# Down projection by Strassen's steps, in two phases of the feed-forward

## The chip, the cores and the metric

One core of a Trainium2 chip. The time is the device time of one execution in microseconds (us), as a median of several runs; the profile is of one execution. TensorE (PE) multiplies matrices, VectorE (DVE), ScalarE (ACT) and GpSimd (POOL) work elementwise, SyncE (SP) issues transfers; GpSimd and ScalarE can issue transfers too.

## The reference

One layer of a streaming encoder on x (512 positions, 1024 features, float32). What the change touches is the channel mixer at its end; everything is float32.

```
x = x + W_o (sigmoid(g_A) * y_A + sigmoid(g_B) * y_B)      # mixer before it
h = rms_norm(x, norm_ffn_g)
up = causal_dwconv(h @ w_up, conv_ffn_w)                   # 1024 -> 2 x 2816, 3 taps
a, b = split(up)
x = x + (silu(a) * b) @ w_down                             # 2816 -> 1024
return rms_norm(x, norm_f_g)
```

## The kernel before

Everything lies transposed: features on the 128 partitions, the 512 positions along the free axis. A matrix is a grid of 128 x 128 blocks; `w_down` has 22 blocks along its 2816 inputs (`k`) and 8 along its 1024 outputs (`j`).

To be exact enough, each float32 operand is split into a high half (rounded to the type that TensorE takes at speed) and a low half, the remainder. `mm3` (lines 175 to 187) forms a product from three matmuls, high by high, low weight by high, high by low, each cut to 256 columns; so a block of 512 positions takes 6 matmuls and one of 256 takes 3. All sums are in PSUM, in eight banks of 512 columns.

Weights come as one stream of chunks, `stream`, each 128 x 1024 at most (8 blocks). `load` issues a chunk's transfer on SP's queue, `AHEAD` chunks ahead of use, into a ring of `AHEAD` + 1 raw buffers. `split` makes the halves: ScalarE copies the raw chunk into the high half (line 154), VectorE subtracts that from the raw chunk (line 158), which is the remainder. There are two buffers for each half, so the split of a chunk waits until TensorE has done with the chunk two before it. `chunk` hands the halves out in order.

A planner (the language's scheduler) sets the order of the instructions on each engine: among those that it expects to be ready, the one that the program has first. It is held by `keep`, which keeps program order for all matmuls and SP's loads, and by `after_split`, which puts a block's instructions behind the last split on their engine.

The feed-forward: the loop over `j` in 0..21 takes two up blocks each (`a` and `b`), multiplies each by the norm's factor (line 724), convolves (`taps`: one scaled copy on ScalarE, two multiply-adds on VectorE), applies silu (line 729), multiplies on GpSimd (line 730), and splits the product into `gh` and `gl` (lines 731 and 732). Then, for each of the 8 output blocks, `down` accumulates 22 blocks from three chunks into one PSUM bank; VectorE adds the bank to `x1` (line 761), ScalarE squares and scales it, GpSimd sums the squares (line 653). The last output block is done in two halves of the positions, so that the first half's norm and output run beside the second half's matmuls (`fin_sum`, `fin_col`, `fin_out`); `warm_on` gives TensorE matmuls without a use while the last norm is worked out.

Of the kernel before, what the change touches and what calls it, by code (L numbers as in the profile page):

```python
# [24 lines left out]
AHEAD = 3  # L25
# [4 lines left out]
PADL, PADR = 48, 120  # L30
# [6 lines left out]
RC = 2 * (S + H)  # L37
WC = D + P
WOFF = {"h": 0, "l": 32}
# [3 lines left out]
def block_kernel(ctx, tc, xT, vecs, wv, win, wmix, wo, wup, wdn, outT):  # L43
# [28 lines left out]
    def col(i):  # L72
        return vec[:, i : i + 1]
# [42 lines left out]
    stream += [(f"up{j}", wup[j], D) for j in range(2 * NP)]  # L116
    for j in range(KB):
        for c in range(3):
            a, b = 8 * c * P, min(8 * c + 8, NP) * P
            stream.append((f"dn{j}{c}", wdn[j, :, a:b], b - a))  # L120
    raws, parts, order = [], [], {}

# [7 lines left out]
    def load(upto):  # L130
        for k in range(len(raws), min(upto, len(stream) - 1) + 1):
            nm, src, ncol = stream[k]
            raw = wp.tile([P, RC], F32, tag="raw", name=f"raw_{nm}", bufs=AHEAD + 1)[:, :ncol]

            keep((nc.scalar if k == 0 else nc.sync).dma_start(raw[:, : VW if k == 0 else ncol], src[:, : VW if k == 0 else ncol]))
            if k == 0:
                keep(nc.sync.dma_start(raw[:, VW:], src[:, VW:]))
            raws.append(raw)

    def split(hl=None):  # L140

        k = len(parts)
        if k == len(stream):
# [3 lines left out]
        hi, lo = hl or [  # L147
            wp.tile([P, WC], F32R, tag=f"w{x}", name=f"w{x}_{nm}", bufs=2)[:, WOFF[x] : WOFF[x] + ncol] for x in "hl"
        ]
        if k == 0:  # L150
            for cs in (slice(0, VW), slice(VW, S + H)):
                keep(nc.vector.tensor_copy(hi[:, cs], raws[k][:, cs]))
        else:
            ins = nc.scalar.activation(hi, raws[k], AF.Copy)  # L154
# [3 lines left out]
        ins = nc.vector.tensor_sub(lo, raws[k], hi.bitcast(F32))  # L158
# [87 lines left out]
    ssq = cp.tile([P, S], F32, tag="ssq", name="ssq1")  # L246
# [398 lines left out]
    ssq2 = cp.tile([P, S], F32, tag="ssq", name="ssq2")  # L645
# [57 lines left out]
    gh = fp.tile([P, NP, S], F32R, tag="gh", name="gh")  # L703
    gl = fp.tile([P, NP, S], F32R, tag="gl", name="gl")

    acc = ring(*range(6))
    rb2 = None
    for j in range(NP):
        uu = []
        if j == 0:  # L710
            nrm = {}

            def mid():
                nrm["c"] = rstd_col([ssq2], NT, 6, "n2")

            def late():
# [179 lines left out]
```

## Time and profile before

| | |
|---|---|
| median of 3 runs | 726.09 us (725.95 to 726.13) |
| the profiled execution | 725.93 us, span 724.1 us |
| mean granted TensorE clock | 0.996 |
| TensorE busy | 715.0 us (99%), 6231 matmuls |
| VectorE, ScalarE, GpSimd busy | 398.6, 293.6, 129.6 us |
| read from HBM, written | 68.29 MB, 2.10 MB |

A row of a group of instructions has the line, the engine, the operation, what is written and read, shapes and count; then the busy time, the mean of one in ns, and the engine's idle time before them with what ended it. A row of the timeline has start and duration in us, then the same, with the idle time before it in brackets. A row of stages has the length, the busy time and count of PE, weight loads (PEld), DVE, ACT and POOL, the granted clock, the busy share of the DMA engines, and GB/s. A row of the chain has start, duration and what ran.

### The profile page before, as it was taken

Reading aid. Unit: us, or ns where it says so; the run is one execution under the profiler, and the core shown is the slowest. Engines: PE = TensorE matmul, PEld = TensorE weight load, DVE = VectorE, ACT = ScalarE, POOL = GpSimd, SP = SyncE. Lnnn points to the kernel's source line nnn. Section 1 sums busy time; section 2 is a strip of 40 time slices with the busy share of each in tenths; the row PEclk is TensorE's granted clock in tenths of the full one; section 3 lists DMA queues with packets and bytes.
Section 4 is the critical chain, followed back from the end, with each engine's and each line's share of the span. In section 5 each row is a group of like instructions: output and inputs, shape, how many; then the busy total and the mean of one; then the engine's idle time right before and its main releaser. Section 6 shows DMA issues by size and latency. Waiting matters only on the chain.

```text
span 724.1 us, 14479 instructions
## 1 busy us (share of the span) xinstructions
PE 715.0 (99%) x6231; PEld 713.5 (99%) x6231; DVE 398.6 (55%) x588; ACT 293.6 (41%) x449; POOL 129.6 (18%) x145
## 2 busy tenths in 40 slices
PE   9999999999999999999999999999999999999996
PEld 9999999999999999999999999999999999999995
DVE  6677767655545445455376666666666663222322
ACT  6564545444332332334254434434434433223321
POOL 5124433222000000123311101101101100000102
PEclk9999999999999999999999999999999999999998
DMA  8523122221232332542233233333333333323303
GB/s 259 156 62 116 61 83 65 61 87 59 65 111 89 106 99 88 162 159 88 88 101 105 88 100 105 90 95 109 89 99 105 89 88 97 110 81 110 103 1 117
DMA packets 23360, 71.39 MB, mean 99 GB/s; under 512 B 2912, under 2 KB 5600, under 8 KB 23296
## 3 DMA queue, kind: packets, MB, share of 16 engines
q1 hardware_dynamic: 20992, 67.09, 30.3%
q0 software_dynamic: 896, 2.13, 0.9%
q10 hardware_dynamic: 1408, 1.24, 0.5%
q8 instruction: 49, 0.80, 0.5%
q14 instruction: 15, 0.12, 0.1%
HBM read 68.29 MB, written 2.10 MB: 97 GB/s over the span
## 4 chain that ended last, share of the span: by engine, by line
PE 95%; DVE 2%; ACT 1%; issue 1%; ACTq 0%; POOL 0%; DVEq 0%
PE p_up L183 33%; PE pd L183 14%; PE p_in L183 14%; PE p_wo L183 6%; PE p_gb L183 5%; PE p_ga L183 5%; PE yc L183 3%; PE ya L183 3%; PE o L183 2%; PE pa L307 2%; PE pb L309 2%; PE tp L473 1%; PE pdB L183 1%; PE pdA L183 1%; PE s L444 1%; PE s L445 1%
## 5 line engine op out<-in xcount | busy, mean ns | idle before, releaser
L183 PE MATMUL p_up<-x1h,wh_up 128*128 128x256 f32 x704 | 137.4, 276 | 0.0
L183 PE MATMUL p_up<-x1h,wl_up 128*128 128x256 f32 x704 | 137.0, 276 | 0.0
L183 PE MATMUL p_up<-x1l,wh_up 128*128 128x256 f32 x704 | 136.9, 276 | 0.0
L183 PEld LDWEIGHTS p_up<-x1h,wh_up 128*128 128x128 f32 x704 | 106.1, 188 | 0.0
L183 PEld LDWEIGHTS p_up<-x1h,wl_up 128*128 128x128 f32 x704 | 105.9, 188 | 0.0
L183 PEld LDWEIGHTS p_up<-x1l,wh_up 128*128 128x128 f32 x704 | 105.9, 188 | 0.0
L158 DVE TENSOR_TENSOR wl_in<-raw_in,wh_in 128x1024 fp32r<-128x1024 f32 x36 | 50.7, 1409 | 30.1 <-ACT wh_in L154 29.6
L730 POOL TENSOR_TENSOR fu<-fu,fu 128x512 f32<-128x512 f32 x22 | 28.4, 1291 | 211.2 <-DVE fu L402 198.3
L158 DVE TENSOR_TENSOR wl_up<-raw_up,wh_up 128x1024 fp32r<-128x1024 f32 x44 | 53.7, 1221 | 14.5 <-ACT wh_up L154 14.5
L183 PE MATMUL pd<-gl,wh_dn 128*128 128x256 f32 x308 | 60.0, 276 | 0.0
L183 PE MATMUL pd<-gh,wh_dn 128*128 128x256 f32 x308 | 60.0, 276 | 0.0
L183 PE MATMUL pd<-gh,wl_dn 128*128 128x256 f32 x308 | 59.9, 276 | 0.0
L183 PE MATMUL p_in<-xgh,wh_in 128*128 128x256 f32 x288 | 56.9, 279 | 1.1 <-DVE t_q L375 1.1
L183 PE MATMUL p_in<-xgl,wh_in 128*128 128x256 f32 x288 | 56.5, 277 | 0.0
L183 PE MATMUL p_in<-xgh,wl_in 128*128 128x256 f32 x288 | 56.4, 277 | 0.0
L158 DVE TENSOR_TENSOR wl_dn<-raw_dn,wh_dn 128x1024 fp32r<-128x1024 f32 (+1 forms) x23 | 26.0, 1132 | 54.9 <-ACT wh_dn L154 54.8
L154 ACT ACTIVATE wh_up<-raw_up 128x1024 fp32r<-128x1024 f32 x44 | 46.4, 1055 | 22.3 <-issue 13.4
L154 ACT ACTIVATE wh_in<-raw_in 128x1024 fp32r<-128x1024 f32 x36 | 38.2, 1060 | 42.5 <-PE ya L183 12.7
L154 ACT ACTIVATE wh_dn<-raw_dn 128x1024 fp32r<-128x1024 f32 (+1 forms) x23 | 22.7, 985 | 66.5 <-PE pd L183 66.1
L183 PEld LDWEIGHTS p_in<-xgh,wh_in 128*128 128x128 f32 x288 | 44.7, 188 | 1.9 <-ACT wh_in L154 1.3
L183 PEld LDWEIGHTS pd<-gl,wh_dn 128*128 128x128 f32 x308 | 46.4, 188 | 0.0
L183 PEld LDWEIGHTS pd<-gh,wh_dn 128*128 128x128 f32 x308 | 46.4, 188 | 0.0
(227 smaller groups left out, 1590.9 us busy)
## 6 DMA issues: line engine op xcount, KB each, us to landing
raw_up<-in_wup_dram SPq DMA_DIRECT2D x44, 512.0 KB, 3.6
raw_in<-in_win_dram SPq DMA_DIRECT2D x36, 512.0 KB, 3.5
raw_dn<-in_wdn_dram SPq DMA_DIRECT2D x16, 512.0 KB, 3.5
raw_mix<-in_wmix_dram SPq DMA_DIRECT2D x8, 512.0 KB, 3.6
raw_wo<-in_wo_dram SPq DMA_DIRECT2D x8, 512.0 KB, 5.6
raw_dn<-in_wdn_dram SPq DMA_DIRECT2D x8, 384.0 KB, 3.2
xr<-in_xT_dram POOLq DMA_DIRECT2D x8, 256.0 KB, 3.8
raw_v<-in_wv_dram SPq DMA_DIRECT2D x7, 260.0 KB, 5.4
```

The source lines that it names most:

```text
L154: ins = nc.scalar.activation(hi, raws[k], AF.Copy)
L158: ins = nc.vector.tensor_sub(lo, raws[k], hi.bitcast(F32))
L183: keep(nc.tensor.matmul(out[:, cs], w, x[:, cs], start=start and i == 0 and c == 0, stop=stop and i == 2 and c == len(cut) - 1,))
L307: keep(nc.tensor.matmul(pa[t][:, :VW], xt, w[:, :VW], start=start, stop=stop))
L309: keep(nc.tensor.matmul(pb[t], xt, w[:, VW:], start=start and t % 2 == 0, stop=stop and t % 2 == 1))
L444: keep(nc.tensor.matmul(s[:, :nn], QT[pr][:, e, qs], KA[pr][:, e, :nn], start=True, stop=False))
L445: keep(nc.tensor.matmul(s[:, :nn], QB[pr % 2][: KR[e], e, qs], KBt[pr % 2][: KR[e], e, :nn], start=False, stop=True))
L473: keep(nc.tensor.transpose(tp[:, ks], pt[:, ks], ident))
L730: nc.gpsimd.tensor_mul(a, a, b)
```

## The change

The feed-forward is done in two phases: hidden blocks 0 to 11, then 12 to 21. In each, the up projection is followed by that part of the down projection, added into `x1` in SBUF.

The down projection takes two output blocks (a pair `i` of rows), two hidden blocks (a pair `q`) and the two halves of the 512 positions as a 2 x 2 matrix product and forms it by seven products of 128 x 128 by 128 x 256 in place of eight, in Winograd's form of Strassen's method. That needs sums on both sides and a recombination:

- Hidden side, `glu`, once per pair `q`: four sums on VectorE (t1 to t4), then one copy and one remainder over all seven operands of 256 columns (eight in phase 1, which also keeps the plain ones).
- Weight side, once per step: five blocks are loaded (320 KB); a DMA issued from GpSimd adds two blocks of 128 KB from HBM onto the fourth and fifth (`add_in`); two GpSimd additions of 128 columns make the sixth and seventh (`sum_up`). `split` calls these one and two chunks ahead.
- Output side, `combine`, once per pair of rows and phase: seven VectorE operations and one ScalarE copy bring four banks' worth of products into two blocks of `x1`. In phase 1 the squares and the scaling follow, the sum of squares now on VectorE.

Phase 0 has 4 x 6 = 24 steps; phase 1 has 3 x 5 = 15, and output blocks 6 and 7 go there without Strassen's method, in three chunks (`dp0` to `dp2`), half by half for the end of the kernel. In each phase the steps of the first two pairs of rows are ordered so that the last two pairs `q` come late. The ring of raw buffers goes from 4 to 5, buffers `fz` from 3 to 2 and `fu` from 4 to 3. The transfer of weights is laid out for this on the host, by copying only.

```diff
-AHEAD = 3
+AHEAD = 4
+PHASES = ((0, 12), (12, NP))
...
+    for ph, (j0, j1) in enumerate(PHASES):
+        qs = list(range(j0 // 2, j1 // 2))
+        head, rest = qs[:-2], qs[-2:]
+        st = [(i, q) for part in (head, rest) for i in (0, 1) for q in part]
+        st += [(i, q) for i in ((2, 3), (2,))[ph] for q in qs]
...
+    def add_in(upto):
...
+                nc.gpsimd.dma_start(form(k, 3, 2), stream[k][1][:, : 2 * P], accum_op=ALU.add)
+    def sum_up(upto):
...
+                add_in(k)
+                nc.gpsimd.tensor_add(form(k, 5), form(k, 3), form(k, 1))
+                nc.gpsimd.tensor_add(form(k, 6), form(k, 5), form(k, 2))
...
     def split(hl=None):
...
         load(k + AHEAD)
+        sum_up(k + 1)
+        add_in(k + 2)
...
+    def glu(ph, j, uu):
...
+        nc.vector.tensor_sub(t1, b11, b12)
+        nc.vector.tensor_sub(t3, b22, b12)
+        nc.vector.scalar_tensor_tensor(t2, t1, -1.0, b22, op0=ALU.mult, op1=ALU.subtract)
+        nc.vector.scalar_tensor_tensor(t4, t2, -1.0, b21, op0=ALU.mult, op1=ALU.subtract)
+        gs, rs = slice(g0, g0 + NF + ph), slice(0, NF + ph)
+        nc.scalar.activation(gh[:, gs, :], graw[:, rs, :], AF.Copy)
+        nc.vector.tensor_sub(gl[:, gs, :], graw[:, rs, :], gh.bitcast(F32)[:, gs, :])
+    PROD = (
+        (1, 0, 2, 0), (2, 1, 0, 0), (6, 2, 0, 1), (0, 6, 1, 0), (3, 3, 1, 1), (5, 4, 2, 1), (4, 5, 3, 0),
+    )
+    def step(ph, i, q, banks, first, last):
+        wh, wl = chunk(f"st{i}_{q}")
...
+        for f, g, b, h in PROD:
...
+            mm3(banks[b][:, th[h]], wh[:, fs], wl[:, fs], gh[:, g0 + g, :], gl[:, g0 + g, :], ...)
...
+        split_next()
+    def split_next():
+        while len(parts) < chunk.n + 1 and len(parts) < len(stream):
+            if stream[len(parts)][0].startswith("dp"):
+                break
+            split()
+    def combine(ph, i, banks):
...
+        nc.scalar.activation(z[:, th[0]], p16[:, th[0]], AF.Copy)
+        nc.vector.tensor_add(m1, p23, m1)
+        nc.vector.tensor_sub(m2, m2, p45)
+        nc.vector.tensor_add(z[:, th[1]], p16[:, th[1]], z[:, th[0]])
+        nc.vector.tensor_add(u3, p7, z[:, th[1]])
+        nc.vector.tensor_add(m1[:, th[1]], p45[:, th[1]], m1[:, th[1]])
+        nc.vector.tensor_add(m1, m1, z)
+        nc.vector.tensor_sub(m2h, m2h, u3.unsqueeze(1).to_broadcast([P, 2, 2 * P]))
...
+    def down(ph, banksets):
...
+            step(ph, i, q, open_[i], first, last)
+            if last:
+                with after_split():
+                    combine(ph, i, open_[i])
...
+    for m in range(2):
+        plain(m, 0, kall)
+    sqA = [fin_sum(0, 0), fin_sum(0, 1)]
+    plain(0, 1, kall[:5])
+    rcA = fin_col(0, sqA)
+    plain(0, 1, kall[5:])
+    fin_out(0, rcA)
+    sqB = [fin_sum(1, 0)]
+    plain(1, 1, kall)
+    sqB.append(fin_sum(1, 1))
```

More of the change, by code (lines that the diff above doesn't have):

```diff
@@ L861, in _layout @@
     wup = np.stack([wup[:NP], wup[NP:]], axis=1).reshape(2 * NP, P, D)
+    wdn = blocks(i["w_down"][0]).reshape(KB, P, NP, P)
+    wst = np.zeros((KB // 2 * (NP // 2), P, 5 * P), f)
+    for a in range(KB // 2):
+        for q in range(NP // 2):
+            w = [wdn[2 * a + m, :, 2 * q + k] for m, k in ((1, 1), (0, 0), (0, 1), (1, 0), (1, 0))]
+            wst[a * (NP // 2) + q] = np.concatenate(w, axis=1)
+    k0, k1 = PHASES[1]
+    wdp = wdn[KB - 2 :, :, k0:k1].transpose(1, 0, 2, 3).reshape(P, -1)
     return {
```

247 lines of the change are left out of this document (154 added, 93 removed).

## The prediction

> **What bounds the kernel now.** First the busy times and the chain of work that ended last (page of the profile, parts 1, 2 and 4), then the chain in order of time, then the stages.
>
> ```profile
> PE 715.0 (99%) x6231; PEld 713.5 (99%) x6231; DVE 398.6 (55%) x588; ACT 293.6 (41%) x449; POOL 129.6 (18%) x145
> PEclk9999999999999999999999999999999999999998
> GB/s 259 156 62 116 61 83 65 61 87 59 65 111 89 106 99 88 162 159 88 88 101 105 88 100 105 90 95 109 89 99 105 89 88 97 110 81 110 103 1 117
> PE 95%; DVE 2%; ACT 1%; issue 1%; ACTq 0%; POOL 0%; DVEq 0%
> ```
> ```profile
> 308.46 43.52 PE p_wo L183 x384
> ...
> 364.67 228.54 PE p_up L183 x2016
> 593.21 104.72 PE pd L183 x924
> ```
> ```profile
> 352.00:593.00 241.00, 241.00 (x2128) 241.00 (x2128) 156.78 (x197) 103.25 (x134) 29.96 (x23) 1.00 0.32 95
> 593.00:698.00 105.00, 105.00 (x929) 105.00 (x929) 31.98 (x33) 30.38 (x37) 10.05 (x6) 1.00 0.30 90
> 698.00:724.10 26.10, 19.15 (x165) 18.67 (x163) 6.68 (x14) 4.73 (x9) 5.41 (x5) 0.90 0.24 82
> ```
>
> TensorE is the chain: 95% of it, at full granted clock (1.00 in both feed-forward stages). The pace is the same everywhere: 104.72/924 = 113.3 ns a matmul in the down projection, 228.54/2016 = 113.4 in the up projection, 43.52/384 = 113.3 before it, whatever bank or operand. So a matmul left out is worth 113.3 ns, if nothing keeps TensorE waiting. In the down stage the others are nearly idle (VectorE 32 of 105 us, ScalarE 30, GpSimd 10). They have to be read by step, not by share, because the new steps are short.
>
> **The change part by part.** All against the profiled execution: 725.93 us (span 724.1), 0.16 below the median of 726.09.
>
> *A, matmuls removed.* Before: 8 x 22 blocks x 6 = 1056. After: 24 steps in phase 0 and 15 in phase 1, each 7 products x 3 = 21, so 819, and 20 blocks x 6 = 120 plain ones: 939. 117 fewer x 113.3 ns = **-13.26 us**. That is the whole gain; a step lasts 21 x 113.3 = 2.38 us.
>
> *The rhythm of a step.* Two buffers hold the split weights, so the chunk of step n+1 is split when TensorE has finished n-1. These rows show that round in the kernel before:
>
> ```profile
> 593.05 0.39 PE L183 MATMUL pd<-gh,wh_dn 128*128 128x256 f32 x2
> 593.16 0.30 PEld L183 LDWEIGHTS pd<-gh,wl_dn 128*128 128x128 f32 x2
> 593.25 0.69 DVE L724 TENSOR_TENSOR fz<-p_up,rb_n 128x512 f32<-128x512 f32 x1 [1.08 <-PE p_up L183]
> 593.25 1.06 ACT L154 ACTIVATE wh_dn<-raw_dn 128x1024 fp32r<-128x1024 f32 x1 [0.36 <-PE p_up L183]
> 593.27 0.39 PE L183 MATMUL pd<-gh,wl_dn 128*128 128x256 f32 x2
> ```
> ```profile
> L154 ACT ACTIVATE wh_dn<-raw_dn x23: 831/1062/1063, 588.2 to 698.0; 128x1024 fp32r<-128x1024 f32 x15, 128x768 fp32r<-128x768 f32 x8
> L158 DVE TENSOR_TENSOR wl_dn<-raw_dn,wh_dn x23: 957/1224/1226, 589.5 to 698.8; 128x1024 fp32r<-128x1024 f32 x15, 128x768 fp32r<-128x768 f32 x8
> ```
> ```profile
> 604.13 1.06 ACT L154 ACTIVATE wh_dn<-raw_dn 128x1024 fp32r<-128x1024 f32 x1 [4.25 <-PE pd L183]
> ...
> 605.22 1.22 DVE L158 TENSOR_TENSOR wl_dn<-raw_dn,wh_dn 128x1024 fp32r<-128x1024 f32 x1 [4.36 <-ACT wh_dn L154]
> ...
> 714.81 0.42 ACT L773 ACTIVATE sq<-x 128x256 f32<-128x256 f32 x1 [3.46 <-DVE x L771]
> ...
> 715.28 0.61 PE L198 MATMUL pc_n<-ones,sq 128*128 128x1 f32 x4 [0.27 <-ACT sq L773]
> ```
>
> The old chunk's successor starts at 593.05, ScalarE's copy at 593.25: 0.20 us. A chunk has now 7 x 128 = 896 columns: between the rows for 768 and 1024 the copy takes 0.95 us and VectorE's remainder 1.09. 604.13 + 1.06 to 605.22 is a hand-over of 0.03, 715.23 to 715.28 one to TensorE of 0.05. Sum 0.20 + 0.95 + 0.03 + 1.09 + 0.05 = 2.32 us, against 2.38 in which the low half's weight load is due (it starts 0.11 before its matmul, which is the step's second). It fits with 0.06 us left; before, a chunk of 8 blocks had 5.44. So whatever VectorE does at the moment when a remainder could start now stops TensorE, and with two buffers nothing is caught up.
>
> *B, the recombination.* `combine` follows the last step of each pair of rows; its VectorE part is seven operations, four of 512 and three of 256 columns. Issue pitch from these rows: 588.29, 588.90, 589.50 give 0.60 for 512; 1.95 for two of 512 and two of 256 leaves 0.37 for 256.
>
> ```profile
> 588.29 0.69 DVE L732 TENSOR_TENSOR gl<-fu,gh 128x512 fp32r<-128x512 f32 x1 [2.16 <-ACT gh L731]
> 588.90 0.69 DVE L724 TENSOR_TENSOR fz<-p_up,rb_n 128x512 f32<-128x512 f32 x1
> 589.50 1.22 DVE L158 TENSOR_TENSOR wl_dn<-raw_dn,wh_dn 128x1024 fp32r<-128x1024 f32 x1
> ...
> 608.21 0.69 DVE L761 TENSOR_TENSOR x<-pd,x 128x512 f32<-128x512 f32 x1 [1.76 <-PE pd L183]
> 609.30 1.23 DVE L158 TENSOR_TENSOR wl_dn<-raw_dn,wh_dn 128x1024 fp32r<-128x1024 f32 x1 [0.40 <-ACT wh_dn L154]
> ...
> 711.39 1.95 DVE L788 TENSOR_TENSOR x<-x,pb_n 128x256 f32<-128x256 f32 x4 [2.27 <-ACT rs L784]
> ```
>
> 4 x 0.60 + 3 x 0.37 = 3.5 us. The code orders it behind the remainder of step n+1, which ends 0.10 us before step n does; the remainder of n+2 stands behind it in the program. The rows at 608.21 show this order: the evacuation and the split are released by the same end of TensorE, and VectorE evacuates first. Then the remainder of n+2 starts at 3.4 us after the end of n and reaches TensorE at 3.4 + 1.09 + 0.05 = 4.55 instead of 2.38: 2.2 us lost. Seven times `combine` runs; after the last of phase 0 comes an up block of 5.44 us, which covers it, after the last of phase 1 the plain part (D). Five x 2.2 = **+10.9**. Bounds: 0, if the remainder goes in between, and 5 x 2.9 = 14.5, if the dependent operations go at their full 0.69 and 0.42 instead of the pitch.
>
> *C, the two ends of the up projection.* The last pair's operands come through a product on GpSimd (1.29 us for 512 columns), four sums (4 x 0.37), one copy of 1792 or 2048 columns (1.7 or 1.9 us by ScalarE's 0.84 ns a column) and a remainder (2.0 or 2.3 by VectorE's 1.05); in the old kernel copy and remainder were 512 wide.
>
> ```profile
> L730 POOL TENSOR_TENSOR fu<-fu,fu 128x512 f32<-128x512 f32 x22 | 28.4, 1291 | 211.2 <-DVE fu L402 198.3 <-ACT fu L729 12.9
> L399 DVE SCALAR_TENSOR_TENSOR fu<-fz,vec,fu 128x511 f32<-128x511 f32 x44 | 33.3, 758 | 1.6 <-ACT fu L398 1.6
> L398 ACT ACTIVATE fu<-fz,vec 128x512 f32<-128x512 f32 x44 | 31.5, 718 | 9.7 <-DVE fz L724 9.6
> ```
>
> They now run beside the first steps. In us after the last up matmul, each behind the chunks that are ready before it: the product with the norm 0.2 to 0.9, the tap on ScalarE to 1.8, two taps on VectorE (0.76 each) 2.2 to 3.7, GpSimd's product, held by a remainder (E), 4.8 to 6.1, the fourth chunk's remainder to 7.1, the sums to 8.5, the copy to 10.3, the long remainder to 12.3, and only then the sixth chunk's, to 13.4, where 12.0 was due: 1.5 us; with 2048 columns 2.0. **+3.5**; bounds 0 (all falls in the gaps) and 7 (the product, too, ahead of a chunk).
>
> *D, the plain part.* The first plain chunk's remainder (1.23 us, 1024 columns) meets the first sum of the last `combine`: 0.6; the third's waits for all of it: 0.5. **+1.1**; 0 to 2.
>
> *E, GpSimd and VectorE.* Each step has two GpSimd additions of 128 columns, and an accumulating DMA of 128 KB that GpSimd issues.
>
> ```profile
> 195.15 1.30 POOL L641 TENSOR_TENSOR g<-g,g 128x512 f32<-128x512 f32 x1 [18.70 <-DVE g L640]
> ...
> 195.35 2.18 DVE L158 TENSOR_TENSOR wl_in<-raw_in,wh_in 128x1024 fp32r<-128x1024 f32 x1 [0.34 <-ACT wh_in L154]
> ```
> ```profile
> L457 POOL TENSOR_SCALAR pp<-pp,m 128x512 f32<-128x512 f32 x8 | 5.5, 693 | 9.6 <-DVE m L456 7.4 <-PE tp L473 2.1
> L457 POOL TENSOR_SCALAR pp<-pp,m 128x128 f32<-128x128 f32 x8 | 3.6, 450 | 7.7 <-DVE m L456 7.5
> ```
> ```profile
> raw_dn<-in_wdn_dram SPq DMA_DIRECT2D x8, 384.0 KB, 3.2
> xr<-in_xT_dram POOLq DMA_DIRECT2D x8, 256.0 KB, 3.8
> ...
> qb<-fr POOLq DMA_DIRECT2D x4, 4.0 KB, 1.7
> ```
>
> The first two rows: a remainder (1.23 alone) that starts while GpSimd works on two inputs takes 2.18, longer by the rest of that work. The new addition lies between a quarter of 1.30, 0.32, and 0.60 (the one-input rows for 128 and 512 columns leave a start of 0.37, and 0.37 + 0.93/4 = 0.60); I take the row of its own width, 0.45. Its place in the step hangs on a chain: a raw buffer is free when a remainder ends (2.28), the load of 320 KB lands 3.05 later (row of 384 KB: 3.2), then the accumulation. No row shows one: it lies between the 1.7 of 4 KB and the 3.8 of 256 KB, by size 2.7, which I take. With three hand-overs of 0.1 the additions begin at 8.33, that is 1.19 into a step, just when a remainder is ready to start. So I take the chance: 0.9 of 2.38 us is adding, a remainder meets one in 0.38 of the steps and waits 0.22: 34 steps beside B's five x 0.085 = **+2.9**; bounds 0 and 34 x 0.45 = 15. The chain itself, 7.1 us with the additions, is covered by five buffers (5 x 2.38 - 2.1 = 9.8) until an accumulation takes 5.4. Behind a waiting addition on GpSimd stand the next accumulation and C's product; behind a load on SP only later loads. Traffic is 448 KB per 2.38 us, 193 GB/s, below the 259 of the first slice.
>
> The Trainium skill (DMA: Bandwidth & Descriptors, section Anatomy of one DMA — SWDGE (gpsimd) path) gives about 2.0 us plus bytes over 436 GB/s for a DMA from GpSimd, as an estimate 2.3 us here; the row of 4 KB (1.7) lies below that line, the row of 256 KB (3.8) above it. By it the additions would begin 0.79 into a step, the first would end 0.05 after the remainder is due, and E would be 34 x 0.05 = 1.7 if the remainder goes ahead of the second addition and 17 if not: a sum of 730 or 745.
>
> *At zero:* the up stage's extra work, per pair four sums (4 x 0.42) and 2.03 us of remainder for 2 x 0.69, is 2.3 us of VectorE, 26 in all on 157 of 241. Its cover is that a chunk there has 5.44 us for 0.20 + 1.06 + 1.23, even with 2.3 in between; without that it would cost as C does, 1.5 for each of nine pairs. The fifth raw buffer moves the first loads by a place: +-0.3. The end after the last matmul has the same chain; one more addition of 256 columns (0.4) is early for one half, and beside 1.7 us of matmuls for the other.
>
> Sum: -13.26 + 10.9 + 3.5 + 1.1 + 2.9 = +5.1: 725.93 + 5.1 = **731**.
>
> **The rivals.** *Faster:* the remainder of n+2 is put ahead of most of `combine`, so B is gone: 725.93 - 13.26 + 7.5 = **720**; with C, D and E also hidden 712.7. For it: a planner sets the order on each engine by when it expects work to be ready, and can leave the code's order: GpSimd issues the last load of x ahead of the first addition to the sum of squares, though the code has six additions before that load.
>
> ```profile
> 320.58 0.54 POOL L689 DMA_DIRECT2D xr<-in_xT_dram  x1 [2.40 <-DVE x L690]
> 321.70 1.28 POOL L653 TENSOR_TENSOR ssq<-ssq,sq 128x512 f32<-128x512 f32 x1 [0.58 <-ACT sq L652]
> ```
>
> Against it: the seven operations are ready first, and at 608.21 the evacuation goes first. It decides from B + C + D + E below 13.26; 0.34. *Even:* the stalls come to 12 to 15 us: 0.09. *GpSimd's queue:* if it has each accumulation directly ahead of its own additions, a step costs 2.7 + 0.9 + 0.2 = 3.8 us: 39 x 1.42 = 55, B shrinks to 5 x 0.75; 725.93 - 13.26 + 55 + 3.8 + 4.6 = **776**. Against it: loads as early as four chunks ahead let two accumulations be under way: 0.07. That the matmuls would not get fewer or would pace otherwise has nothing for it in three stages of 113.3.
>
> **How the numbers follow.** 0.50 for my forecast (728 to 742), 0.34, 0.09 and 0.07 as above. 0.2% is about what a measurement of this kernel tells from no change (1.5 us). Faster 0.34, same 0.09, slower 0.57. The range goes from 714 (nearly all hidden) to 746 (E at its upper end): it leaves out some 0.06 below and 0.10 above, the queue rival among it.
>
> **What would show it.** A: 939 matmuls in the down parts at 113.3. B: five waits of TensorE on VectorE's remainder of 2.2 us, each behind a `combine`. C: waits of 1.5 to 2 some 12 us into each phase's steps. E: remainders of more than 1.09 us beside GpSimd additions. Wrong if TensorE waits under 10 us in all (faster), or if GpSimd's additions wait for accumulations and steps last near 3.8 (far slower).

## The result and the profile after

The changed kernel takes 779.4 us (median; 777.3 to 782.1) beside 726.0 us for the kernel before on the same chip: 1.0737 times as long, 95% interval 1.0695 to 1.0779. I had forecast 731 and a range up to 746. The rival that ends at 776, GpSimd's queue, had a chance of 0.07.

First the lines of the page of the profile after that answer to those of before: busy times, the granted clock in 40 slices, the chain, of the groups the two kinds of matmul that waited longest (busy time, mean of one in ns, then the idle time before them), the remainder and the copy, and the two transfers of a step (KB, us from issue to landing).

```profile
PE 726.3 (94%) x6114; PEld 716.5 (92%) x6114; DVE 467.5 (60%) x690; ACT 316.3 (41%) x465; POOL 200.6 (26%) x256
...
PEclk9999999999999999999999999997899999999998
...
PE 65%; DVE 9%; DMA 8%; POOL 7%; issue 6%; ACT 5%; SPq 0%; DVEq 0%; POOLq 0%; ACTq 0%
...
L235 PE MATMUL p_up<-x1h,wl_up 128*128 128x256 f32 x704 | 139.5, 280 | 14.4 <-DVE wl_up L210 14.4
...
L235 PE MATMUL dn<-gh,wl_st 128*128 128x256 f32 x273 | 82.2, 301 | 18.4 <-DVE wl_st L210 18.4
...
L210 DVE TENSOR_TENSOR wl_st<-raw_st,wh_st 128x896 fp32r<-128x896 f32 x39 | 44.3, 1142 | 47.8 <-ACT wh_st L206 47.8
...
L206 ACT ACTIVATE wh_st<-raw_st 128x896 fp32r<-128x896 f32 x39 | 37.1, 952 | 80.2 <-POOL raw_st L182 47.8
...
raw_st<-in_wst_dram SPq DMA_DIRECT2D x39, 320.0 KB, 2.9
raw_st<-in_wst_dram POOLq DMA_DIRECT2D x39, 128.0 KB, 3.2
```

The chain, 95% TensorE before, now runs through every engine: 35% of it is VectorE, DMA, GpSimd, issue and ScalarE. The matmuls wait for the remainders, the remainders for the copies, and the copies for GpSimd's second addition (47.8 us). The view of waits goes one link further (us in total, times, longest):

```profile
POOL raw_st L181 <- DMA raw_st<-in_wst_dram: 79.9, 39, 3.5
...
PE dn L235 <- DVE wl_st L210: 18.4, 18, 2.0
...
PE p_up L235 <- DVE wl_up L210: 14.4, 9, 2.4
```

GpSimd's first addition waits for its accumulating DMA in every one of the 39 steps, 79.9 us in all. The stages, in time order: up projection and steps of phase 0, the same of phase 1; the last row is the last 16 steps of phase 0 alone.

```profile
364.51:494.93 130.42, 123.13 (x1059) 121.96 (x1058) 91.02 (x117) 53.93 (x64) 24.70 (x26) 0.99 0.30 90
494.93:579.76 84.83, 69.18 (x506) 64.89 (x505) 44.16 (x54) 26.23 (x30) 40.09 (x58) 0.92 0.53 128
579.76:699.44 119.68, 111.92 (x963) 110.93 (x961) 81.34 (x104) 46.60 (x54) 22.07 (x23) 0.99 0.32 90
699.44:749.76 50.32, 41.63 (x318) 39.90 (x316) 33.47 (x42) 22.92 (x30) 22.22 (x33) 0.93 0.46 112
517.98:579.76 61.78, 49.24 (x338) 45.49 (x337) 29.49 (x39) 16.40 (x20) 26.90 (x43) 0.89 0.54 130
```

At 113.36 ns a matmul (228.54/2016, the up projection before), their 1056, 504, 960 and 315 matmuls would take 119.7, 57.1, 108.8 and 35.7 us, 321.4 together; they take 385.25. So 63.9 us are lost, 42.3 in the steps and **21.6 in the up projections**, where I had priced nothing. A step lasts 61.78/16 = 3.86 us and not 2.38. With 13.26 us of matmuls removed and 0.8 us elsewhere, that is the rise of the span from 724.1 to 775.5, 51.4 us.

Two stretches of the timeline show the two mechanisms. In the steps (TensorE's rows left out):

```profile
510.35 0.46 POOL L181 TENSOR_TENSOR raw_st<-raw_st 128x128 f32<-128x128 f32 x1 [1.85 <-DMA raw_st<-in_wst_dram]
510.83 0.88 POOL L173 DMA_DIRECT2D raw_st<-in_wst_dram  x1
510.85 0.95 ACT L206 ACTIVATE wh_st<-raw_st 128x896 fp32r<-128x896 f32 x1 [3.23 <-POOL raw_st L181]
511.43 0.77 POOL L182 TENSOR_TENSOR raw_st<-raw_st 128x128 f32<-128x128 f32 x1
511.83 1.32 DVE L210 TENSOR_TENSOR wl_st<-raw_st,wh_st 128x896 fp32r<-128x896 f32 x1 [2.38 <-ACT wh_st L206]
...
514.05 0.46 POOL L181 TENSOR_TENSOR raw_st<-raw_st 128x128 f32<-128x128 f32 x1 [1.85 <-DMA raw_st<-in_wst_dram]
```

The accumulation of the next step is issued at 510.83, behind an addition that itself waited for the accumulation before. Its first addition starts at 514.05, 3.22 us later, and the next issue follows that. One accumulation is under way at a time: a round of 514.05 - 510.35 = 3.70 us, whatever TensorE does. So it is for 34 of the 38 accumulations after the first: they are issued when the one before has landed. In the up projection (VectorE and ScalarE):

```profile
405.03 0.43 DVE L791 TENSOR_TENSOR graw<-graw 128x256 f32<-128x256 f32 x1 [1.47 <-POOL graw L786]
...
406.17 0.68 DVE L775 TENSOR_TENSOR fz<-p_up,rb_n 128x512 f32<-128x512 f32 x1
406.35 1.71 ACT L795 ACTIVATE gh<-graw 128x1792 fp32r<-128x1792 f32 x1 [4.88 <-DVE graw L793]
...
408.09 2.02 DVE L796 TENSOR_TENSOR gl<-graw,gh 128x1792 fp32r<-128x1792 f32 x1 [1.23 <-ACT gh L795]
408.57 1.04 ACT L206 ACTIVATE wh_up<-raw_up 128x1024 fp32r<-128x1024 f32 x1
...
410.69 1.22 DVE L210 TENSOR_TENSOR wl_up<-raw_up,wh_up 128x1024 fp32r<-128x1024 f32 x1
```

VectorE stands 1.47 us in front of the second of the sums, because GpSimd's product is not done, and 1.23 us in front of the long remainder, because ScalarE's copy of 1792 columns is not. ScalarE stands too: 4.88 us in front of that long copy, until the sums are done. The copy of the next weights, behind it in ScalarE's queue, could have started at about 405.24, for TensorE went on to the next chunk at 405.04 and the copy follows by 0.20 us where no pair's work is in the way (399.60 and 399.80, a chunk earlier). It starts at 408.57, 3.3 us late, and the weights' remainder, behind the long remainder and a tap, 1.1 us after its copy, at 410.69. That is 4.4 us late, against a cover of 5.44 - 0.20 - 1.06 - 1.23 = 2.95 us, the cover on which I had booked the extra work at zero.

### The profile page after: what moved, and what is told of

Read it like the earlier page. It is cut to its first block, busy times and chain, and to the rows that moved or that the text cites. A ratio compares the mean times of both kernels' runs of the same rounds, so it can differ in the third digit from the quotient of the medians.

```text
span 775.5 us, 14650 instructions
## 1 busy us (share of the span) xinstructions
PE 726.3 (94%) x6114; PEld 716.5 (92%) x6114; DVE 467.5 (60%) x690; ACT 316.3 (41%) x465; POOL 200.6 (26%) x256
## 3 DMA queue, kind: packets, MB, share of 16 engines
q1 hardware_dynamic: 23584, 69.65, 28.4%
## 4 chain that ended last, share of the span: by engine, by line
PE 65%; DVE 9%; DMA 8%; POOL 7%; issue 6%; ACT 5%; SPq 0%; DVEq 0%; POOLq 0%; ACTq 0%
PE p_up L235 16%; PE p_in L235 13%; DMA raw_st<-in_wst_dram 7%; PE p_wo L235 6%; PE p_ga L235 5%; PE p_gb L235 5%; DVE wl_up L210 3%; PE yc L235 3%; PE ya L235 3%; ACT gh L795 2%; PE o L235 2%; POOL graw L786 2%; PE dn L235 2%; POOL raw_st L181 2%; DVE fu L451 2%
## 5 line engine op out<-in xcount | busy, mean ns | idle before, releaser
L235 PE MATMUL p_up<-x1h,wl_up 128*128 128x256 f32 x704 | 139.5, 280 | 14.4 <-DVE wl_up L210 14.4
L235 PE MATMUL dn<-gh,wl_st 128*128 128x256 f32 x273 | 82.2, 301 | 18.4 <-DVE wl_st L210 18.4
L235 PE MATMUL dn<-gh,wh_st 128*128 128x256 f32 x273 | 80.8, 296 | 6.0 <-ACT wh_st L206 5.9
L235 PE MATMUL dn<-gl,wh_st 128*128 128x256 f32 x273 | 79.6, 292 | 0.0
L235 PEld LDWEIGHTS dn<-gh,wl_st 128*128 128x128 f32 x273 | 55.5, 203 | 22.5 <-DVE wl_st L210 22.5
L786 POOL TENSOR_TENSOR graw<-fu,fu 128x512 f32<-128x512 f32 x22 | 29.0, 1318 | 175.6 <-DVE fu L454 162.8
L210 DVE TENSOR_TENSOR wl_st<-raw_st,wh_st 128x896 fp32r<-128x896 f32 x39 | 44.3, 1142 | 47.8 <-ACT wh_st L206 47.8
L206 ACT ACTIVATE wh_st<-raw_st 128x896 fp32r<-128x896 f32 x39 | 37.1, 952 | 80.2 <-POOL raw_st L182 47.8
L235 PEld LDWEIGHTS dn<-gh,wh_st 128*128 128x128 f32 x273 | 55.4, 203 | 7.9 <-ACT wh_st L206 7.9
L235 PEld LDWEIGHTS dn<-gl,wh_st 128*128 128x128 f32 x273 | 55.4, 203 | 0.0
```

Source lines behind the costliest of these rows:

```text
L206: ins = nc.scalar.activation(hi, raw, AF.Copy)
L210: ins = nc.vector.tensor_sub(lo, raw, hi.bitcast(F32))
L235: keep(nc.tensor.matmul(out[:, cs], w, x[:, cs], start=start and i == 0 and c == 0, stop=stop and i == 2 and c == len(cut) - 1,))
L786: nc.gpsimd.tensor_mul(dst, a.rearrange(halves_of, h=2), b.rearrange(halves_of, h=2))
```

## The experiments

Theory: GpSimd's queue sets the steps, the order on VectorE and ScalarE the up stage, and `combine` and the phase starts the rest. Rivals: the accumulating transfer or the additions are too dear by themselves, `combine` alone is the loss, or the clock does it. All ratios are to the kernel before. The table has the stages in us and the mean of the last 16 steps of phase 0; at the pace of before the row would read 119.7, 57.1, 108.8, 35.7, 2.38.

| run | median | ratio (95%) | up 0 | steps 0 | up 1 | steps 1 | step |
|---|---|---|---|---|---|---|---|
| changed kernel | 779.4 | 1.0737 (1.0695 to 1.0779) | 130.4 | 84.8 | 119.7 | 50.3 | 3.86 |
| e1 | 744.9 | 1.0251 (1.0235 to 1.0266) | 129.4 | 65.0 | 116.4 | 42.0 | 2.71 |
| e2 | 760.5 | 1.0475 (1.0460 to 1.0491) | 129.3 | 73.0 | 116.3 | 48.2 | 2.90 |
| e3 | 779.4 | 1.0738 (1.0693 to 1.0784) | 130.5 | 84.3 | 118.0 | 51.4 | 3.82 |
| e4 | 790.6 | 1.0884 (1.0866 to 1.0902) | 130.7 | 91.0 | 121.3 | 56.0 | |
| e5 | 769.5 | 1.0604 (1.0587 to 1.0622) | 121.9 | 89.3 | 113.4 | 51.0 | |
| e6 | 763.1 | one run | 130.1 | 74.9 | 118.7 | 46.5 | 3.24 |
| e7 | 727.9 | 1.0023 (1.0014 to 1.0032) | 119.8 | 64.3 | 109.5 | 42.2 | 2.67 |
| e8 | 746.7 | 1.0280 (1.0265 to 1.0296) | 119.9 | 75.5 | 109.5 | 48.8 | 3.10 |
| e9 | 768.3 | 1.0575 (1.0556 to 1.0594) | 125.8 | 79.5 | 116.9 | 54.9 | |
| e10 | 721.7 | 0.9935 (0.9921 to 0.9948) | 119.8 | 59.8 | 109.4 | 39.8 | 2.38 |
| e11 | 789.0 | 1.0873 (1.0849 to 1.0898) | 132.3 | 88.9 | 122.1 | 53.9 | 3.76 |
| e12 | 743.3 | 1.0236 (1.0221 to 1.0251) | 119.8 | 69.5 | 109.5 | 52.3 | 2.72 |
| e13 | 745.8 | 1.0272 (1.0255 to 1.0289) | 119.8 | 71.8 | 109.5 | 53.0 | 2.48 |
| e14 | 754.1 | 1.0385 (1.0369 to 1.0400) | 122.0 | 74.9 | 111.7 | 52.1 | 2.86 |
| e15 | 728.8 | 1.0034 (1.0021 to 1.0048) | 119.9 | 63.3 | 109.3 | 42.4 | 2.47 |
| e16 | 723.5 | 0.9961 (0.9948 to 0.9975) | 119.8 | 61.5 | 109.4 | 40.8 | 2.51 |

Of the times expected below, e2, e4, e5, e7, e8, e9, e13 and e14 ended outside every range named for them, e10 and e12 by 0.7 and 1.3 us. The readings therefore go by the stages, not by the totals. e1, e6, e7, e10, e12 and e13 leave out all or part of the weight sums, so their result is not the layer's.

**e1, the weight side's sums left out.**

```diff
+                if nm.startswith("st"):
+                    keep(nc.sync.dma_start(raw[:, 5 * P : 7 * P], src[:, : 2 * P]))
...
-        return k < len(stream) and stream[k][0].startswith("st")
+        return False
```

> The changed kernel without GpSimd's part of a step: the four sums of weight blocks are left out (neither the accumulating DMA nor the two additions), and the same 128 KB come in by a second plain load on SP into the last two blocks, so that bytes, splits and matmuls stay. GpSimd's loop (accumulate 3.2, add 0.46, hand over, next: 3.7 us a step) as the cause of the long steps: the steps fall from 135 us to 39 x 2.38 = 93 plus the stalls behind combine and at the phase starts (up to 14), so 93 to 107, and the kernel from 779 to about 740 to 752. Combine and the buffers as the cause (the forecast's B and C): those stay, 779 falls by no more than E's 3. The clock gate (TensorE's pace doubled after waits) would go with the waits, in either case.

The last 16 steps of phase 0:

```profile
515.78:559.20 43.42, 39.04 (x339) 38.45 (x337) 27.43 (x37) 16.49 (x20) 0.00 (x0) 1.00 0.57 175
```

61.8 us become 43.4, with the clock back at 1.00. In all four stages 32.5 us go, 28.1 of them in the steps. 31 us remain above the pace: 17.2 in the up stages, and in the steps five waits for a remainder behind `combine` (1.85, 1.17, 1.85, 1.85, 1.12 us) and the phase starts.

**e2, accumulations issued a step earlier, with GpSimd's order held.**

```diff
-        add_in(k + 2)
+        add_in(k + 3)
...
+                keep(nc.gpsimd.dma_start(form(k, 3, 2), ..., accum_op=ALU.add))   # both additions too
```

> All the work stays; on GpSimd's queue each accumulating DMA is ordered one step earlier, ahead of the previous chunk's additions, so that it flies while they run. If the order in the queue is the cause, a step no longer costs 3.2 + 0.46 + hand-overs: the steps fall to 95 to 112 us, the kernel to 740 to 757, near the run without sums, with E's collisions (0 to 5 us) between them. If accumulations themselves cannot follow each other faster than one in 3.2 us (they take turns on the queue or at the memory), a step stays at 3.3 or more: 779 falls by 6 at most.

The step falls from 3.86 to 46.36/16 = 2.90 us, with the same transfers, additions and buffers:

```profile
520.93:567.29 46.36, 41.56 (x339) 40.38 (x337) 29.96 (x39) 16.66 (x20) 30.56 (x43) 0.96 0.73 173
```

Of the 38 accumulations after the first, 29 are now issued while the one before is in flight, and 4 were before. So most of it was the order on GpSimd's queue. The held order has a price at each phase's start, a wait of 4.30 us: the additions of the first steps stand behind the last pair's product, which waits for the last taps.

```profile
497.62 1.25 POOL L786 TENSOR_TENSOR graw<-fu,fu 128x512 f32<-128x512 f32 x1 [6.14 <-DVE fu L454]
498.85 0.44 POOL L181 TENSOR_TENSOR raw_st<-raw_st 128x128 f32<-128x128 f32 x1
```

**e3, `combine` behind the split of step n+2.**

```diff
             if last:
+                split_next(2)
                 with after_split():
```

> The seven operations of combine are ordered on VectorE behind the remainder of the step after next; nothing else changes. If combine's place is a cost of its own (the forecast: 5 x 2.2 us), 779 falls by 8 to 11 to about 769. If GpSimd's loop sets the rhythm of 3.7 us a step, the remainder had 1.3 us to spare and waits for its weights anyway: within 3 us of 779.

No change. This is the order on which my rival "Faster" rested. While GpSimd sets the round, `combine`'s place costs nothing and saves nothing.

**e4 and e5, two ways of ordering the up stage.** e4 puts the next chunk's split ahead of the norm's product; e5 puts the sums, the long copy and the long remainder behind the next block's split.

```diff
+                while len(parts) < chunk.n + 2 and stream[len(parts)][0].startswith("up"):   # e4
+                    split()
```
```diff
+        if j + 1 < PHASES[ph][1]:           # e5: run in the next up(), after its split()
+            pend.extend((sums, hi_lo))
```

> In the up projection the remainder of the next weight chunk is ordered ahead of the scaling with the norm, the taps and the work on the hidden tiles, as the kernel does in its first part; the steps are untouched. If the 21 us by which the up projection is longer than 2016 matmuls come from VectorE's order (the remainder behind the long remainder of the hidden tiles and a tap, 1.3 to 2.5 us for each pair, and TensorE's half pace after it), they go but for 2 to 6: about 760 to 764. If the extra work does not fit beside the splits at any order (VectorE or ScalarE too full), 779 falls by under 6.

> In the up projection the four sums, the copy and the long remainder of a finished hidden pair are ordered behind the next two weight splits, not where the pair ends; the steps are untouched. If the up projection is longer because VectorE and ScalarE, in order, stand at the pair's chain (sums waiting 1.5 us for GpSimd's product, the long remainder 1.2 us for its copy) while the weight split is behind it, the nine waits of 1.3 to 2.5 us go, and the stage falls from 250 to 229 to 234 us: the kernel to 760 to 766. If the work does not fit at any order, the waits move to other chunks, as they did when the split was ordered ahead of the norm's product alone: 775 to 792.

e4 made it worse. Its timeline shows the weight remainder still behind the sum that waits for the product:

```profile
407.69 0.42 DVE L795 TENSOR_TENSOR graw<-graw 128x256 f32<-128x256 f32 x1 [1.47 <-POOL graw L790]
...
408.82 1.22 DVE L210 TENSOR_TENSOR wl_up<-raw_up,wh_up 128x1024 fp32r<-128x1024 f32 x1
```

ScalarE's copy of these weights had ended at 405.60, so VectorE stood idle in front of the sum with the remainder's operands ready behind it. Here the split followed the pair's sums, since `glu` had run before it. e5 moves the sums, the long copy and the long remainder instead, and the first up stage falls to within 2.2 us of the pace:

```profile
365.03:486.91 121.88, 120.13 (x1059) 119.93 (x1058) 93.83 (x117) 53.26 (x63) 24.96 (x24) 1.00 0.33 93
```

Both up stages give 14.9 us; the steps take back 5.2. As e5 moves ScalarE's and VectorE's work together, it does not tell their shares apart.

**e6, the accumulation replaced by a plain copy from the same queue.**

```diff
-                nc.gpsimd.dma_start(form(k, 3, 2), ..., accum_op=ALU.add)
+                nc.gpsimd.dma_start(form(k, 3, 2), ...)
```

> The DMA of 128 KB that GpSimd issues only copies, it does not add (the first sum of the blocks is left out). If its 3.2 us are the price of a DMA that GpSimd issues, it stays at 3.0 to 3.3 and the kernel at 779 +- 6. If adding in memory is what makes it longer than the 2.7 that I took by size, it falls to 2.3 to 2.8, and as 39 steps hang on it serially, the kernel by 15 to 30.

```profile
raw_st<-in_wst_dram POOLq DMA_DIRECT2D x39, 128.0 KB, 2.5
```
```profile
518.45:570.35 51.90, 43.75 (x338) 42.18 (x337) 28.60 (x37) 16.65 (x20) 24.12 (x43) 0.93 0.49 150
```

It lands in 2.5 us where the accumulation takes 3.2, and the step goes from 3.86 to 3.24 us: 0.62 for 0.7. By this one run the landing counts almost whole. By the fit in the Trainium skill (DMA: Bandwidth & Descriptors, section Anatomy of one DMA — SWDGE (gpsimd) path) 128 KB take an estimated 2.3 us. The plain copy agrees with it within 0.2 us; the accumulation takes 0.9 us more.

**e7, no weight sums, the up stage as in e5, `combine` as in e3.**

> The run without GpSimd's sums of weights, with combine behind the split and the hidden pair's work deferred, so that of the forecast's terms A and the starts of the phases (C) are left. From 744.9: combine's five stalls of 1.9 go (9), and the up projection's 17 but for 0 to 5: 718 to 724, that is below the kernel before (726). If the stalls only trade places (VectorE or ScalarE full), 730 to 745.

The up stage stands at the pace (119.82 of 119.82 busy in the first row), and with e1 that makes the up stage's order 9.6 + 6.9 = 16.5 us. The steps do not:

```profile
364.38:484.20 119.82, 119.82 (x1059) 119.82 (x1058) 92.75 (x117) 53.67 (x64) 14.25 (x11) 1.00 0.32 97
...
505.79:548.49 42.70, 38.98 (x339) 38.39 (x338) 27.20 (x37) 16.20 (x19) 0.00 (x0) 1.00 0.58 178
```

`combine` behind the split of n+2 still leaves waits of 1.86, 0.49, 1.86, 2.07 and 1.12 us. It now delays the remainder of n+3, and with 0.06 us to spare in a step, nothing catches up before it.

**e8, all of it with the sums in place**, accumulations issued four chunks ahead and additions two, GpSimd's order held.

> All the work of the change, in better orders: each accumulation two chunks ahead of its additions on GpSimd's queue, the last pair's product behind the additions that the first steps need, combine behind the split, the hidden pair's work deferred. If the change's loss is one of orders alone, it comes within E of the run without sums: 722 to 732. If GpSimd's additions beside VectorE's remainders cost much by themselves (each 0.46 alone, up to 1.2 when they meet), 732 to 745.

```profile
510.64:560.22 49.58, 42.37 (x339) 40.73 (x337) 31.67 (x38) 16.20 (x19) 35.06 (x42) 0.97 0.66 159
```

The up stages are clean and the time is 33 us below the changed kernel's, but a step takes 3.10. In this kernel the load lands in 3.9 and the accumulation in 3.6 us, so the chain from a free buffer to the sums has grown.

**e9, the two additions on VectorE.**

```diff
-                nc.gpsimd.tensor_add(form(k, 5), form(k, 3), form(k, 1))
+                nc.vector.tensor_add(form(k, 5), form(k, 3), form(k, 1))   # the second too
```

> All the work of the change; the two additions of weight blocks go from GpSimd to VectorE, behind each remainder (two of 128 columns, some 0.25 us each, in the 1.29 that VectorE has free in a step), GpSimd's queue holds accumulations alone (0.88 of issue each), combine comes in three pieces behind three successive steps, the hidden pair's work is deferred. If the cost of the sums lies in GpSimd's queue and its turns with VectorE, the steps fall to 93 to 100 us and the kernel to 718 to 729: level with the kernel before, or below. If the accumulations land too late for VectorE, which then stands in order before the next remainder, 735 to 750.

A miss, outside both ranges. At the phase starts a weights' remainder now stands on VectorE behind the last hidden tile's scaling and taps, and another behind the long remainder, with waits from 3.65 to 4.63 us there, and both transfers land later (accumulation 3.5, load 4.4).

**e10, as e7, with `combine` in three pieces, one behind each of three splits.**

```diff
+        keep(nc.vector.tensor_add(m1, p23, m1))
+        keep(nc.vector.tensor_add(z[:, th[1]], p16[:, th[1]], z[:, th[0]]))
+        yield                                  # next piece behind the next split
```

> The sums of weight blocks left out as in the first run, and combine in three pieces behind three successive steps instead of in one. The run with combine as one piece behind the split (727.9) still had its five waits of 1.9. If a step has 1.29 us of VectorE free and combine's 3.5 only has to be spread over three of them, 9 us go: 717 to 721, and what is left above 713 is the start of the phases. If the wait is one for combine's results or banks and not for VectorE's time, it stays at 725 to 728.

```profile
506.08:544.16 38.08, 38.08 (x339) 38.08 (x337) 27.65 (x37) 16.49 (x20) 0.00 (x0) 1.00 0.69 199
```

16 steps in 38.08 us, 2.38 each, TensorE never waiting. `combine` as one block cost 6.8 us of stages (e7 to e10). In three pieces it is hidden, because each fits into the 2.38 - 1.09 = 1.29 us that VectorE has free in a step. This kernel, without the weight sums, is faster than before, by 0.65% (0.52 to 0.79%).

**e11, the changed kernel with six matmuls without a use in most steps.**

```diff
+            for _ in range(6):
+                keep(nc.tensor.matmul(banks[3][:, th[1]], gh[:, g0, :P], gl[:, g0, :], start=False, stop=False))
```

> The changed kernel with six added matmuls of 256 columns (6 x 0.113 = 0.68 us, into half a bank that nothing reads) behind each step but the last of a pair of rows, where TensorE waits for 1 to 2 us. The granted clock was 0.92 and 0.93 in the two stretches of steps. If waits make TensorE run at half pace for 3 us afterwards and that lies on the path, the clock goes to 0.99 and the time falls by 3 to 8 to 771 to 776. If the rhythm is GpSimd's alone, the clock rises and the time stays at 779 +- 3. If the fillers lie on the path, up to 32 x 0.68 = 22 us more.

```profile
497.09:586.00 88.91, 76.94 (x627) 73.49 (x625) 43.07 (x54) 26.14 (x30) 40.21 (x59) 1.00 0.53 123
```

The clock in phase 0's steps goes from 0.92 to 1.00, and the last 16 take 3.76 us each beside 3.86, with 6 x 0.113 = 0.68 us more work in most of them. So in those steps the matmuls are not on the path, and half pace costs at most 1.7 us of the 61.8. The last nine steps of phase 1 fall from 31.8 to 28.4 us; whether half pace is the reason there is open. The time as a whole rises by 9.6 us: in the profiled executions the first eight and the first six steps, where TensorE does not yet wait, take 5.8 and 6.9 us more, and the up stages 1.9 and 2.4.

**e12 and e13, one half of the weight sums at a time, on e10.** e12 has the accumulations, with a ScalarE copy in place of the additions; e13 the additions without the accumulations.

```diff
+                keep(nc.scalar.activation(form(k, 5, 2), form(k, 3, 2), AF.Copy))   # e12
-                nc.gpsimd.dma_start(form(k, 3, 2), ..., accum_op=ALU.add)           # e13
```

> The run without sums (721.7), with the accumulating DMAs put back (two chunks ahead of their use) in place of the second plain load; the two additions are left out, a copy of 256 columns on ScalarE (0.37 us of the 1.4 free) waits for the accumulation where they would. If the accumulation's time is the rest of the cost (load 3.9 + accumulation 3.5 against three steps of 2.38), steps grow by 0.3 to 0.5: 733 to 742. If it is hidden by the buffers, as the forecast had it, 721 to 726.

> The run without sums (721.7), with GpSimd's two additions a step put back in place of the second plain load, the accumulations left out (the additions take the blocks as loaded). By term E of the forecast: 2.9 us more (0 to 15), 722 to 727. If additions and remainders in turn fill a step (1.09 + 0.46 + 0.46 and hand-overs of a lock on top), the steps grow to 2.6 and more: 730 to 737.

```profile
510.09:553.55 43.46, 39.86 (x339) 38.68 (x337) 27.59 (x37) 21.31 (x34) 10.35 (x12) 1.00 0.73 180
```
```profile
516.41:556.13 39.72, 39.59 (x338) 38.76 (x337) 29.11 (x37) 16.56 (x20) 12.61 (x25) 1.00 0.55 152
```

Over e10, e12 loses 22 us in the steps and e13 25. In the 16 steps above a step costs (43.46 - 38.08)/16 = 0.34 us more with accumulations and 0.10 more with additions, 5.4 and 1.6 us. The rest lies elsewhere. The first eight steps of phase 0 and six of phase 1, at whose start the last pair's work meets the first steps, cost e12 4.3 and 5.1 us more than e10, and e13 10.3 and 9.8: e13 has four waits of 4.3 to 5.0 us there, for a weights' remainder that stands on VectorE behind the last hidden tile's taps or behind the long remainder, as in e9. That is a price of e13's order, not of additions. In the last nine steps of phase 1, e12 loses another 7.3 us and e13 3.4. In e12 ScalarE stands 2.59 us there in front of the copy that waits for an accumulation, and then does 2.3 us of squares and scaling before the next weights' copy (696.78 to 699.37). So part of this comes from the stand-in on ScalarE; how much is open.

**e14, e9 with the starts reordered.**

> All the work of the change with the additions on VectorE (0.29 us each behind a remainder) as in e9, and at each phase's start the first two weight splits ahead of the last hidden pair's work, so that the waits of 4 us there, and TensorE's half pace after them, go (some 30 of e9's 768). If the steps then run at 2.38, 722 to 728, level with the kernel before; if the accumulations land too late for VectorE in order, steps of 2.6 to 2.9 and 732 to 745.

```profile
515.83:561.56 45.73, 40.81 (x339) 39.05 (x337) 34.16 (x65) 16.66 (x20) 10.36 (x12) 1.00 0.72 171
```

14 us better than e9, and 2.86 us a step. Moving the additions does not help as long as the accumulations stay: a step is no shorter than e12's 2.72, and waits of 5.29 and 5.78 us at the starts remain.

**e15 and e16, the whole work without accumulating DMAs.** The two blocks that the DMA adds lie in the buffer already (the first two of the five), so one VectorE addition of 256 columns does it, 0.42 us. `combine` goes in up to five pieces, the last pair's sums, copy and remainder in four; e16 also puts the last taps and the product behind splits, and spreads the squares.

```diff
-                nc.gpsimd.dma_start(form(k, 3, 2), ..., accum_op=ALU.add)
+                order_sum(k, nc.vector.tensor_add(form(k, 3, 2), form(k, 3, 2), form(k, 0, 2)))
...
+            for n, f in ((3, sums_a), (4, sums_b), (5, lambda: hl_part(0, 4)), (6, lambda: hl_part(4, NF + ph))):
+                while len(parts) < chunk.n + n:
+                    split()
```

> The whole work of the change without accumulating DMAs: VectorE adds the first two blocks (one operation of 256 columns, 0.42 us, behind each remainder), GpSimd makes its two additions as before, two chunks ahead; combine in five pieces, and the last hidden pair's work of each phase in four, each behind a weight split. If the accumulations were the larger part of the rest, the steps between run at 2.4 to 2.5 us as in e13 (2.48) and the kernel comes to 724 to 734. If VectorE's 1.51 and GpSimd's 0.92 us a step, in turns, fill the 2.38 and more, the steps go to 2.6 to 2.8 and the kernel to 736 to 745.

> e15 (728.8) still had waits of 2.0 to 3.2 us at the third step of each phase, where scaling and taps of the last hidden tile stand ahead of a weight split, 1.5 at the second combine of the second phase and 0.6 and 1.7 at the plain chunks. The taps, the sums and the copies of the last pair are each put behind one more split, the two combines of the second phase end with the steps, their squares come one a step, and the plain chunks' remainders go ahead of the last combine's rest. If VectorE's free time in a step (0.87 us beside the remainder and the addition) is what places cost, 5 us go and some 2 come back: 723 to 727, level with the kernel before or below it. If turns with GpSimd take the free time, 727 to 731.

Busy times, chain and the last 16 steps of phase 0 of e16:

```profile
PE 707.8 (98%) x6114; PEld 703.4 (97%) x6114; DVE 488.8 (68%) x728; ACT 316.5 (44%) x467; POOL 179.8 (25%) x220
...
PE 88%; DVE 8%; ACT 2%; DMA 1%; issue 0%; SPq 0%; POOL 0%; DVEq 0%; ACTq 0%
```
```profile
505.74:545.83 40.09, 39.90 (x339) 39.08 (x337) 34.35 (x52) 16.47 (x20) 16.27 (x29) 1.00 0.51 151
```

e16 forms all that the changed kernel forms in 723.5 us, 0.39% (0.25 to 0.52%) under the kernel before: faster than both, by more than the 0.2% that a measurement tells from none. VectorE has the addition as well and is 68% busy. Of the 13.26 us of matmuls some 3 are kept. The stages still hold 119.8 + 61.5 + 109.4 + 40.8 - 321.4 = 10.1 us above the pace, nearly all in the steps.

## Why the prediction was wrong

Where the 63.9 us went, by differences between kernels: the weight sums with GpSimd's queue 32.5 (changed kernel to e1), the up stage's order 16.5 and next to nothing from `combine`'s place (e1 to e7, 17.0 in all), `combine` as one block 6.8 (e7 to e10), and 7.6 that e10 still has, mostly at the starts. The split depends on the order of removal: e3 shows that `combine` costs nothing while GpSimd sets the round.

- **A, right.** Every stage without a wait runs at the old pace: e10's 16 steps at 38.08/336 = 113.3 ns, e7's up stage at 119.82. A matmul left out was worth its 113 ns, and a step is 2.38 us.
- **E, the failing step.** The sentence "loads as early as four chunks ahead let two accumulations be under way" is about buffers. The queue decided: `split` calls the additions of k+1 ahead of the accumulation of k+2, and GpSimd takes at least the first of them in that order (510.35, 510.83), so an accumulation is issued only after the one before has landed. E itself says that the next accumulation stands behind a waiting addition, and still counts with two under way. The rival had the right queue: I had written it out and then argued it away with the wrong resource. e2 shows it: the same work, issued a step earlier, and 3.86 becomes 2.90.
- **The rival "GpSimd's queue", right mechanism, numbers by luck.** Its step of 3.8 us is 2.7 + 0.9 + 0.2; the quoted round of 3.70 is 3.22 from issue to use and one addition of 0.46, for the second does not lie in the round. Its 776 puts 55 us of loss on the queue and nothing on the up stage; measured are 42.3 in all the steps, of which the first of each phase still run at 2.38, and 21.6 in the up stages. The two errors cancel.
- **E, the sizes.** The landing of 2.7 us is near a plain copy's (2.5 in e6) and too low for an accumulation (3.2 to 3.6). The collisions of additions and remainders, 2.9 us forecast, come to an estimated 4 (39 steps at e13's 0.10). What the formula for the covered chain missed is what accumulations cost even in e12's order: 0.34 us a step, an estimated 13 us over 39 steps. "Covered until an accumulation takes 5.4" did not hold; that the load before it got slower (3.9 us in e8, 3.05 assumed) may be part of it, and the rest stays open, as does why accumulations and additions together (3.10 us a step in e8) cost more than the two apart.
- **"At zero", a second failing step, wrong by 16.5 to 21.6 us.** I added VectorE's work, 2.3 us a pair, against 5.44 us of cover. The sum was right and the question wrong. An engine in order also loses what it waits for in front of an instruction, and ScalarE, which I left out, loses most: in the pair shown the weights' copy is 3.3 us late behind the long copy, and their remainder another 1.1 on VectorE. My price without the cover, 1.5 for each of nine pairs, 13.5, would have been nearer.
- **B, right mechanism, over-sized.** Five waits behind `combine` are there in e1, 7.8 us together instead of 10.9.
- **C, under-sized; D, no wait in the changed kernel.** For C 3.5 us were forecast; e10 still loses 2.7 and 3.2 in the first eight and first six steps of the phases. For D it was 1.1; TensorE does not wait in the changed kernel's plain part, and once for 1.0 us in e10's.
- **The rival "Faster", wrong mechanism.** Putting the remainder of n+2 ahead of `combine` frees nothing (e3, e7). Dividing it over three steps does (e10).
- **The clock** stood in neither sum nor rivals. In the starts of the changed kernel's 2,931 matmuls of up projection and steps, 30 intervals above 1 us hold 43 us more than the pace, and some 150 of 0.18 to 0.24 us, which is half pace, another 15. e11 shows for the last 16 steps of phase 0 that hardly any of this is a loss of its own there; elsewhere it is not shown.

## What to carry to other kernels

Write out the queue of the slowest-answering engine for one round, issue and use in program order, before pricing its transfers: a DMA issued behind the consumer of the one before has its whole latency in the round, however many buffers there are. Where the main engine has a few hundredths of a microsecond to spare in a step, an off-path block is not hidden by being moved, only by being cut to the free time of each step. And check the cover of in-order work on every engine that takes part, by what each instruction waits for, not by the sum of busy times.

## What the runs showed of the hardware

- **Accumulating costs 0.7 us on a 128 KB DMA** from GpSimd: 3.2 us to landing against 2.5 for the plain copy (e6). Its issue has a row of 0.88 us on GpSimd, of which the next addition's row overlaps the last 0.28 (510.83 and 511.43 above).
- **TensorE falls to half pace after a wait of about 2 us.** A wait is here the time between the starts of two matmuls, less the 0.113 us of the pace. The first row is the changed kernel after a wait of 2.38 us, the second e10 after one of 1.81:

```profile
482.55:486.17 3.62, 3.62 (x19) 3.62 (x20) 3.58 (x5) 1.24 (x2) 0.24 (x1) 0.57 0.37 106
```
```profile
666.28:669.50 3.22, 3.22 (x28) 3.22 (x29) 0.94 (x1) 0.63 (x1) 0.00 (x0) 1.00 0.61 183
```

  Over the up stages and steps of the changed kernel and the experiments, take the waits from 1 us up with no other above 0.3 us in the 5 us before or the 3 us behind. None of 87 below 1.9 us was followed by half pace, 7 of 20 from 1.9 to 2.2, 12 of 14 from 2.2 to 3, and 14 of 15 above. Half pace lasts 2 to 5.5 us at 0.21 us a matmul, so a wait just above the mark costs an estimated 1 to 2.6 us more. The Trainium skill (TensorE: Matmul & The Clock Gate, Part 1: The HAM clock gate) puts the fall after at least one idle window of about 3.4 us; here 2.2 us were enough in most cases, and the measurement decides.
- **VectorE's remainders stretch beside GpSimd's additions**: 1.32 us instead of 1.09 in the round above. In e13, where GpSimd issues no accumulation, 15 of the steps' remainders have no work of GpSimd beside them and take 1.08 or 1.09 us; the other 24 have a median of 1.23. Over a step that was only 0.10 us. The 0.77 us of the addition at 511.43 is something else: six additions of the changed kernel's trace that follow an issue, with no work of VectorE beside them, take 0.75 to 0.77 us as well, and 27 with neither take 0.45 or 0.46.
